# Mixer of a decoder trunk: the exponentials of the first query block turned by VectorE and sixteen DMAs

## The chip, the cores and the metric

One Trainium2 chip, one of its cores. The metric is the device time of one execution in microseconds; lower is better. The kernel before takes 979.72 us (median of 3 runs, 979.69 to 980.86).

## The reference, cut to what matters

The model is two layers of SwiGLU, mixer, SwiGLU over 256 positions of width 1024, all in float32. Only the mixer's dilated half is touched. For each of 8 heads of width 64 it is, as the kernel computes it in one piece:

```python
s = (q @ k.T) / sqrt(64) + log(multiplicity of the key in three dilated windows)   # -inf where none
p = exp(s - max(s))
o = (p @ v) / sum(p)
```

Queries come in two blocks of 128. Block 0 sees keys 0 to 127 (8 tiles of 128x128 exponentials, one per head), block 1 sees keys 0 to 255 (16 tiles). TensorE wants the exponentials with the keys on the partitions for the product with v, so each 128x128 tile has to be turned.

## The kernel before, in words

Weights come in loads of 1 MB (`load`, lines 240, 247, 233), all issued from SyncE's queue into three rotating buffers named raw. ScalarE casts each half of a load to a high part (`hi`, lines 272 and 276), VectorE subtracts to get a low part (`lo`, lines 272 and 277; at two places GpSimd does), and TensorE multiplies in three passes. One `tick` is one such split, of half a load.

The mixer first projects: 96 steps (`STEPS`) of TensorE matmuls (lines 700 to 702 and 305 to 307, output pj_m), six chunks of 16 steps, then the out-projection as steps 96 and up. All other work is hung behind these steps by hand in the table `PLAN`; the order on TensorE, VectorE and ScalarE is exactly the order of the program. The order on SyncE's queue is not written by hand: a scheduler sets it when the program is built, from priorities and from when it believes a transfer's buffer is free. A load is asked for by the first tick that needs it. In the mixer's second half these are the ticks of steps 50, 58, 65 and 73 for the last four loads of w_in (each serves two ticks: 50 and 53, 58 and 61, 65 and 68, 73 and 75), and steps 83, 92, 98 and 101 for w_out.

Around the change: `scores` (line 763) and `expos` (lines 779, VectorE, and 780, ScalarE) make exponentials of block 1 at step 36 and of block 0 at step 46. Block 1 is turned without TensorE: `flip` (line 817) transposes every 32x32 square in place on VectorE, at steps 44 and 47, and `carry` (line 827) moves the squares to their places by 16 DMAs between SBUF addresses, at steps 48 to 63. Block 0 is turned at step 53 by `turn_p`: eight TensorE transposes (line 810) into two PSUM tiles and two ScalarE copies (line 812). Both results are read by `attend_dil` (line 857), block 0 first at step 94. Between them lie `rope` at steps 56 and 64 (lines 728 to 730), the scores of the differential half at steps 68 and 75, their exponentials in `expos`, `differ` (lines 789 to 797) and `turn_p` of that half at steps 77 to 83.

SBUF is given out by hand in rooms: exponentials of the dilated half lie in E (block 0) and B (block 1), those of the differential half in E (block 0) and A (block 1), the turned tiles in F and C. Room D holds the rotated q and k of the differential half.

Of the kernel before, what the change touches and what calls it, by code (L numbers as in the profile page):

```python
# [11 lines left out]
F32 = mybir.dt.float32  # L12
# [8 lines left out]
P = 128  # L21
# [6 lines left out]
NH_DIL = 8  # L28
# [3 lines left out]
NT = S // P  # L32
# [13 lines left out]
def _two_pi_parts():  # L46
# [18 lines left out]
PLAN = {  # L65
    8: "tick",
    10: "norm",
    11: "tick tick",
    13: "tick",
    16: "table",  # L70
    17: "rope,0,0 rope,0,1",
    19: "tick",
    21: "tick",
# [5 lines left out]
    35: "tick",  # L79
    36: "score,dil,1 exp,dil,1,0 exp,dil,1,2 exp,dil,1,1 exp,dil,1,3",  # L80
    40: "rope,2,0",
    44: "flip,0 flip,2",
    43: "tick",
    45: "tick",
    46: "score,dil,0 exp,dil,0,0 exp,dil,0,2 exp,dil,0,1 exp,dil,0,3",
    47: "flip,1 flip,3",
    48: "rope,2,1",
    50: "tick",
    53: "turnp,dil,0,0 turnp,dil,0,1 tick",
    56: "rope,3,0",  # L90
    58: "tick",
    61: "tick",
# [32 lines left out]


for _n in range(16):
    PLAN[48 + _n] = f"{PLAN.get(48 + _n, '')} carry,{_n}"


@with_exitstack
def trunk_kernel(ctx: ExitStack, tc: tile.TileContext, a: dict, out: bass.AP):
    nc = tc.nc
# [11 lines left out]
    def trb(name):  # L145
        return pp.tile([P, 512], F32, tag="tr", name=name, bufs=2)
# [4 lines left out]
    def room(tag, shape, dt, name):  # L151

        return big.tile([P, *shape], dt, tag=f"room{tag}", name=name)
# [514 lines left out]
    def mixer(l, nx, cs, consts, nxt):  # L668
        nm = f"m{l}"
# [17 lines left out]
        vs, es, dens, PT, prs, mrg, pjs, outs, scs, qk = ({} for _ in range(10))  # L687
# [44 lines left out]
        def late(t):  # L732

            if "late" not in prs:
                prs["late"] = room("B", [4, 512], F32, f"late_{nm}")
            return prs["late"][:, t]
# [29 lines left out]
        def expos(fam, t, i):  # L766

            nk = (t + 1) * P
            mask = consts[f"mask_{fam}"]
            if (fam, t) not in es:  # L770
                es[fam, t] = room("EB"[t] if fam == "dil" else "EA"[t], [8, nk], F32, f"ex{fam}{t}_{nm}")
                if fam == "dif":
                    dens[t] = spool.tile([P, 8], F32, tag="den", name=f"den{t}_{nm}", bufs=2)
            s3, mk = scs.pop((fam, t, i)), mask[:, (2 - t - 1) * P:]
            mx = spool.tile([P, 2], F32, tag="mx", name=f"mx{fam}{t}{i}_{nm}", bufs=4)
            for g in range(2):
                h = 4 * g + i
                e = expo_of(fam, t, h)
                V.tensor_tensor_reduce(e, s3[:, g], mk, -(HD ** -0.5), 3e38, ALU.add, ALU.min, mx[:, g:g + 1])
                A.activation(e, e, AF.Exp, bias=mx[:, g:g + 1], scale=-1.0,  # L780
                             accum_out=dens[t][:, h:h + 1] if fam == "dif" else None)

        def expo_of(fam, t, h):
            return es[fam, t][:, h]
# [14 lines left out]

        def turn_p(fam, t, b, copies="a"):  # L800

            heads = range(NH_DIL) if fam == "dil" else range(0, 8, 2)
            if (fam, t) not in prs:
                prs[fam, t] = room("FC"[t], [2 * (t + 1), 512], F32, f"PTdil{t}_{nm}") if fam == "dil" else None
            o = prs[fam, t][:, b] if fam == "dil" else late(t + b)
            o = o.rearrange("p (k c) -> p k c", c=P)
            blocks = [(h, kt) for h in heads for kt in range(t + 1)][4 * b:4 * b + 4]
            tp = trb(f"trp{fam}{t}{b}_{nm}")
            for i, (h, kt) in enumerate(blocks):
                T.transpose(tp[:, i * P:(i + 1) * P], expo_of(fam, t, h)[:, kt * P:(kt + 1) * P], ident)  # L810
                PT[fam, t, h, kt] = o[:, i]
            COPY[copies](o, tp.rearrange("p (k c) -> p k c", c=P))

        def flip(i):

            e = es["dil", 1][:, i::4]
            V.transpose(e, e)

        def carry(n):

            if not n:
                prs["dil", 1] = room("C", [2 * NH_DIL, P], F32, f"PTdil1_{nm}")
                for b in range(2 * NH_DIL):
                    PT["dil", 1, b // 2, b % 2] = prs["dil", 1][:, b]
            f, t = n // 4, n % 4
            e = es["dil", 1].rearrange("p h (k c) -> p (h k) c", c=P)
            nc.sync.dma_start(prs["dil", 1][t * 32:(t + 1) * 32, :, f * 32:(f + 1) * 32],
                              e[f * 32:(f + 1) * 32, :, t * 32:(t + 1) * 32])

        def attend_dif(t):  # L830
            p3 = outs["ps", t] = scb(f"avf{t}_{nm}").rearrange("p (h e) -> p h e", e=2 * HD)
# [36 lines left out]
        def merge(fam, t):  # L868
# [12 lines left out]
            else:  # L881
                A.activation(mh, t3, AF.Copy, scale=gain[:, 0:1])
                V.scalar_tensor_tensor(ml, t3, gain[:, 0:1], mh.bitcast(F32), op0=ALU.mult, op1=ALU.subtract)

        JOBS = {"norm": nx.scale, "table": tables, "rope": rope, "score": scores, "exp": expos, "differ": differ,
                "turnp": turn_p, "value": value, "avdif": attend_dif, "avdil": attend_dil, "ndif": norm_dif,
                "ndil": norm_dil, "flip": flip, "carry": carry,
                "merge": merge, "tick": lambda low="v": ticks(1, low)}

# [172 lines left out]
```

## Time and profile before

| | us |
|---|---|
| median of 3 runs | 979.72 |
| the profiled execution | 979.83 |
| its span, first to last instruction | 978.0 |
| TensorE busy | 967.5 (99%) |
| VectorE busy | 713.4 (73%) |
| ScalarE busy | 550.8 (56%) |
| DMA queue of the loads and carries, share of 16 engines | 57.9% |

All rows come from the one profiled execution. Each row gives the start in us from the span's start, then the duration, the engine, the line and what the instruction writes and reads. Matmuls are pipelined, so a matmul's cost in a stream is the distance of its start from the next one's, not its duration. The first layer's mixer runs its second half from about 236 to 290 us, the second layer's from about 716 to 770 us.

### The profile page before, as it was taken

To read this page: it belongs to the slowest core of one execution; us is meant where nothing else is said; L and a number is where in the kernel's file an instruction comes from. 1 tells how busy PE (TensorE), PEld (TensorE's weight loads), DVE (VectorE), ACT (ScalarE), POOL (GpSimd) and SP (SyncE) were. 2 spreads that over 40 slices of the span, in tenths; PEclk is the share of its full clock that TensorE was granted. 3 is DMA by queue.
4 is the path that set the end of the run, shared out by engine and by line. 5 is a ranking of instruction groups with operands and counts; after the bars stand their busy time and mean duration, and the time that the engine had idled before them with its cause. 6 is when DMAs were issued, how large, how long until landed. Compare 5 with 4: busy or idle time off the path is not lost.

```text
span 978.0 us, 15500 instructions
## 1 busy us (share of the span) xinstructions
PE 967.5 (99%) x5947; PEld 854.2 (87%) x5947; DVE 713.4 (73%) x1290; ACT 550.8 (56%) x982; POOL 57.1 (6%) x63
## 2 busy tenths in 40 slices
PE   8999999999999999999999999999999999999997
PEld 7888888899888888888888888889998988888886
DVE  6887788689668877775478777665986789777542
ACT  7765655355656665564357656554447566665532
POOL 0000000010212000000010000001002120000000
PEclk9999999999999999999999999999999999999999
DMA  9965566635635666466646566653654656855531
GB/s 291 274 213 187 158 197 205 215 127 160 189 112 179 205 207 202 163 209 199 215 151 193 174 194 204 206 192 110 215 143 135 197 173 190 240 174 199 188 130 44
DMA packets 159691, 179.96 MB, mean 184 GB/s; under 512 B 30288, under 2 KB 122624, under 8 KB 159616
## 3 DMA queue, kind: packets, MB, share of 16 engines
q1 hardware_dynamic: 159440, 178.69, 57.9%
q8 instruction: 47, 0.77, 0.3%
q10 hardware_dynamic: 176, 0.27, 0.1%
q14 instruction: 28, 0.23, 0.1%
HBM read 174.75 MB, written 1.05 MB: 180 GB/s over the span
## 4 chain that ended last, share of the span: by engine, by line
PE 92%; DVE 4%; ACT 2%; issue 1%; DMA 0%; SPq 0%; POOLq 0%; POOL 0%; ACTq 0%
PE u_f L373 8%; PE g_f L373 8%; PE dnf L373 8%; PE u_s L373 8%; PE g_s L373 7%; PE g_f L370 4%; PE u_f L370 4%; PE dnf L370 4%; PE dns L373 4%; PE u_s L370 4%; PE g_s L370 4%; PE pj_m L700 3%; PE pj_m L701 3%; PE pj_m L702 3%; PE dns L370 2%; DVE lo L277 2%
## 5 line engine op out<-in xcount | busy, mean ns | idle before, releaser
L277 DVE TENSOR_TENSOR lo<-raw,hi 128x1024 fp32r<-128x1024 f32 (+1 forms) x293 | 353.5, 1225 | 134.7 <-ACT hi L276 133.8
L276 ACT CAST hi<-raw 128x1024 fp32r<-128x1024 f32 (+1 forms) x297 | 303.4, 1046 | 124.3 <-PE u_f L373 26.8
L373 PE MATMUL u_s<-xs_s,hi 128*128 128x512 f32 x352 | 127.3, 395 | 0.0
L373 PE MATMUL g_s<-xs_s,hi 128*128 128x512 f32 x352 | 127.0, 394 | 0.0
L370 PE MATMUL g_s<-xs_s,lo 128*128 128x256 f32 x352 | 91.7, 281 | 0.0
L370 PE MATMUL u_s<-xs_s,lo 128*128 128x256 f32 x352 | 91.5, 280 | 0.0
L373 PEld LDWEIGHTS u_s<-xs_s,hi 128*128 128x128 f32 x352 | 66.0, 187 | 11.2
L373 PEld LDWEIGHTS g_s<-xs_s,hi 128*128 128x128 f32 x352 | 66.0, 188 | 11.0
L700 PE MATMUL pj_m<-xs_m,hi 128*128 128x256 f32 x256 | 72.8, 284 | 0.0
L702 PE MATMUL pj_m<-xs_m,lo 128*128 128x256 f32 x256 | 71.6, 280 | 0.0
L701 PE MATMUL pj_m<-xs_m,hi 128*128 128x256 f32 x256 | 71.6, 280 | 0.0
L370 PEld LDWEIGHTS g_s<-xs_s,lo 128*128 128x128 f32 x352 | 66.5, 189 | 3.9
L370 PEld LDWEIGHTS u_s<-xs_s,lo 128*128 128x128 f32 x352 | 66.5, 189 | 3.9
L373 PE MATMUL g_f<-xs_in,hi 128*128 128x512 f32 x176 | 65.1, 401 | 0.0
L373 PE MATMUL u_f<-xs_in,hi 128*128 128x512 f32 x176 | 64.8, 400 | 0.0
L373 PE MATMUL u_f<-xs_f,hi 128*128 128x512 f32 x176 | 63.7, 395 | 0.0
L373 PE MATMUL g_f<-xs_f,hi 128*128 128x512 f32 x176 | 63.5, 394 | 0.0
L700 PEld LDWEIGHTS pj_m<-xs_m,hi 128*128 128x128 f32 x256 | 48.1, 188 | 1.0 <-issue 0.7
L701 PEld LDWEIGHTS pj_m<-xs_m,hi 128*128 128x128 f32 x256 | 48.2, 188 | 0.1
L702 PEld LDWEIGHTS pj_m<-xs_m,lo 128*128 128x128 f32 x256 | 48.1, 188 | 0.0
L272 ACT CAST hi<-raw 128x1024 fp32r<-128x1024 f32 x32 | 31.5, 1046 | 25.5 <-PE pj_m L701 9.3
L272 DVE TENSOR_TENSOR lo<-raw,hi 128x1024 fp32r<-128x1024 f32 x32 | 38.4, 1235 | 10.3 <-ACT hi L272 10.3
(361 smaller groups left out, 2203.6 us busy)
## 6 DMA issues: line engine op xcount, KB each, us to landing
raw<-in_ffn_gate_dram SPq DMA_DIRECT2D x86, 512.0 KB, 4.1
raw<-in_ffn_up_dram SPq DMA_DIRECT2D x86, 512.0 KB, 5.2
raw<-in_ffn_down_dram SPq DMA_DIRECT2D x41, 1024.0 KB, 5.1
raw<-in_w_in_dram SPq DMA_DIRECT2D x24, 1024.0 KB, 5.2
raw<-in_w_out_dram SPq DMA_DIRECT2D x8, 1024.0 KB, 6.3
raw<-in_ffn_down_dram SPq DMA_DIRECT2D x6, 512.0 KB, 3.6
PTdil_m<-exdil_m SPq DMA_DIRECT2D x32, 64.0 KB, 2.3
xt<-turned SPq DMA_DIRECT2D x16, 64.0 KB, 5.2
```

The costliest lines, as they stand in the source:

```text
L272: out = [lambda: A.copy(hi, raw), lambda: ENGINE[low].tensor_sub(lo, raw, hi.bitcast(F32))]
L276: out.append(lambda sl=sl: A.copy(hi[:, sl], raw[:, sl]))
L277: out.append(lambda sl=sl: ENGINE[low].tensor_sub(lo[:, sl], raw[:, sl], hi[:, sl].bitcast(F32)))
L370: T.matmul(ps[:, :S], wl, xs[:, 0], start=False, stop=False)
L373: T.matmul(ps, wh, xs.rearrange("p j s -> p (j s)"), start=start, stop=stop)
L700: T.matmul(ps, hi, nx.xs[k][:, 0], start=k == 0, stop=False)
L701: T.matmul(ps, hi, nx.xs[k][:, 1], start=False, stop=False)
L702: T.matmul(ps, lo, nx.xs[k][:, 0], start=False, stop=k == KD - 1)
```

## The change

Block 0 of the dilated exponentials is turned as block 1 is. `turnp,dil,0,0` and `turnp,dil,0,1` leave step 53; two flips of four heads each come in at step 54; sixteen carries of block 0 come in at steps 64 to 79 (those of block 1 stay at 48 to 63). The exponentials of the differential block 0 move from room E to room D, since room E is now read by the carries until they are done. `flip` and `carry` take the block as an argument, and `turn_p` keeps only the differential half.

```diff
-    53: "turnp,dil,0,0 turnp,dil,0,1 tick",
+    53: "tick",
+    54: "flip,0,0 flip,0,1",
...
 for _n in range(16):
-    PLAN[48 + _n] = f"{PLAN.get(48 + _n, '')} carry,{_n}"
+    for _t in range(NT):
+        PLAN[64 - 16 * _t + _n] = f"{PLAN.get(64 - 16 * _t + _n, '')} carry,{_t},{_n}"
...
-                es[fam, t] = room("EB"[t] if fam == "dil" else "EA"[t], [8, nk], F32, f"ex{fam}{t}_{nm}")
+                es[fam, t] = room("EB"[t] if fam == "dil" else "DA"[t], [8, nk], F32, f"ex{fam}{t}_{nm}")
...
+        def flip(t, i):
+
+            e = es["dil", t][:, i::4] if t else es["dil", t][:, 4 * i:4 * i + 4]
             V.transpose(e, e)
...
+        def carry(t, n):
 
             if not n:
+                prs["dil", t] = room("FC"[t], [NH_DIL * (t + 1), P], F32, f"PTdil{t}_{nm}")
+                for b in range(NH_DIL * (t + 1)):
+                    PT["dil", t, b // (t + 1), b % (t + 1)] = prs["dil", t][:, b]
+            f, to = n // 4, n % 4
+            e = es["dil", t].rearrange("p h (k c) -> p (h k) c", c=P)
+            nc.sync.dma_start(prs["dil", t][to * 32:(to + 1) * 32, :, f * 32:(f + 1) * 32],
+                              e[f * 32:(f + 1) * 32, :, to * 32:(to + 1) * 32])
```

A carry of block 0 moves 32 partitions x 8 heads x 32 elements, 32 KB in runs of 128 bytes; one of block 1 moves twice as much.

## Rows read from the trace of the kernel before

**Rows 1.** The page: busy time by engine, and the chain that ended last.

```profile
PE 967.5 (99%) x5947; PEld 854.2 (87%) x5947; DVE 713.4 (73%) x1290; ACT 550.8 (56%) x982; POOL 57.1 (6%) x63
...
PE 92%; DVE 4%; ACT 2%; issue 1%; DMA 0%; SPq 0%; POOLq 0%; POOL 0%; ACTq 0%
```

**Rows 2.** Busy time in one stretch: PE, PEld, DVE, ACT, POOL, clock, DMA, GB/s.

```profile
236.00:290.00 54.00, 54.00 (x387) 47.28 (x386) 36.51 (x88) 29.91 (x65) 8.65 (x6) 1.00 0.51 149
```

**Rows 3.** TensorE in order of time at step 53; then all transposes of line 810.

```profile
237.37 0.28 PE L701 MATMUL pj_m<-xs_m,hi 128*128 128x256 f32 x1
237.49 0.28 PE L702 MATMUL pj_m<-xs_m,lo 128*128 128x256 f32 x1
...
238.60 0.28 PE L701 MATMUL pj_m<-xs_m,hi 128*128 128x256 f32 x1
...
L810 PE MATMUL trpdil_m<-ident,exdil_m x16: 271/272/273, 237.6 to 718.7; 128*128 128x128 f32 x16
```

**Rows 4.** By tile: flips, with ns min/median/max, first and last start.

```profile
L817 DVE STREAM_TRANSPOSE exdil_m<-exdil_m x8: 669/688/709, 230.2 to 715.3; 128x512 f32<-128x512 f32 x8
```

**Rows 5.** ScalarE in order of time, with the idle before and its releaser.

```profile
238.24 1.07 ACT L812 COPY PTdil_m<-trpdil_m 128x512 f32<-128x512 f32 x2 [1.85 <-PE trpdil_m L810]
239.20 2.96 ACT L276 CAST hi<-raw 128x1024 fp32r<-128x1024 f32 x3
```

**Rows 6.** VectorE in order of time, steps 50 to 64.

```profile
237.47 1.22 DVE L277 TENSOR_TENSOR lo<-raw,hi 128x1024 fp32r<-128x1024 f32 x1
240.29 1.23 DVE L277 TENSOR_TENSOR lo<-raw,hi 128x1024 fp32r<-128x1024 f32 x1 [1.61 <-ACT hi L276]
241.44 0.68 DVE L728 TENSOR_TENSOR qkdif_m<-pj_m,csr_m 128x512 f32<-128x512 f32 x1
...
247.04 1.53 DVE L730 TENSOR_TENSOR qkdif_m<-qkdif_m,turn_m 128x512 f32<-128x512 f32 x1
```

**Rows 7.** TensorE in order of time: the scores of step 68.

```profile
249.11 2.01 PE L763 MATMUL scdif_m<-qkdif_m 32*128 32x256 f32 x32
```

**Rows 8.** SyncE's queue in order of time: carries, the next load, both layers.

```profile
235.72 11.88 SPq L827 DMA_DIRECT2D PTdil_m<-exdil_m  x16
247.70 0.57 SPq L240 DMA_DIRECT2D raw<-in_w_in_dram  x1
...
716.01 10.71 SPq L827 DMA_DIRECT2D PTdil_m<-exdil_m  x16
```

**Rows 9.** SyncE's queue at the start of the span: small transfers back to back.

```profile
1.73 0.43 SPq L233 DMA_DIRECT2D raw<-in_ffn_up_dram  x1
2.21 0.43 SPq L916 DMA_DIRECT2D xt<-in_x_dram  x1
```

**Rows 10.** By line: loads of w_in, all 24, from issue to landing.

```profile
DMA to landing us min/median/max: 5.0/5.2/7.0
```

**Rows 11.** SyncE's queue in the last up-projection: groups of four like carries, and loads.

```profile
822.27 2.69 SPq L558 DMA_DIRECT2D xt<-turned  x4
825.85 0.37 SPq L233 DMA_DIRECT2D raw<-in_ffn_gate_dram  x1
...
826.81 3.58 SPq L558 DMA_DIRECT2D xt<-turned  x4
...
834.32 0.37 SPq L233 DMA_DIRECT2D raw<-in_ffn_gate_dram  x1
...
835.29 6.11 SPq L558 DMA_DIRECT2D xt<-turned  x4
```

**Rows 12.** The chain from step 73's cast: ScalarE, VectorE, TensorE.

```profile
256.13 1.03 ACT L276 CAST hi<-raw 128x1024 fp32r<-128x1024 f32 x1
...
257.82 1.22 DVE L277 TENSOR_TENSOR lo<-raw,hi 128x1024 fp32r<-128x1024 f32 x1
...
263.83 0.73 PE L810 MATMUL trpdif_m<-ident,exdif_m 128*128 128x128 f32 x4
```

**Rows 13.** TensorE in order of time: the first reader of block 0's turned tiles.

```profile
275.68 0.78 PE L857 MATMUL avl_m<-vdil_m,PTdil_m 128*128 128x65 f32 x6
```

## What I predicted before seeing the change

> **What bounds the kernel now.** I read the page first: TensorE is busy for 967.5 us of a span of 978.0, and 92% of the chain that ended last is TensorE's [rows 1]. [...] So a microsecond taken from TensorE's stream is a microsecond of the kernel, if nothing that TensorE reads comes later than it does now. The other rows are for that "if": who hands TensorE its operands, and how much time each has to spare.
>
> **What goes.** The eight transposes of step 53. One ordinary matmul starts 0.12 us after the other (237.37, 237.49); across the transposes the second matmul behind starts at 238.60 [rows 3]. That is 1.11 us where two ordinary distances would be 0.24, so the transposes cost 0.87 us. Sixteen transposes in all [rows 3], eight in each layer: 1.74 us of TensorE. The matmul behind them waits for nothing else there, so I count all of it. With them go two ScalarE copies, 1.07 us, and the 1.85 us that ScalarE stood still ahead of them for TensorE [rows 5].
>
> **What VectorE gets.** Two flips per layer of 128x512, as wide as those of block 1, at 0.69 us [rows 4]: 1.38 us, at step 54. VectorE is in order, and behind the flips stand the rope of step 56, two splits, the rope of step 64 and, at TensorE, the scores of step 68, which read both ropes. The flips are covered by VectorE's idle 1.61 us ahead of the split at 240.29 [rows 6]. That idle comes from ScalarE's cast, which started only at 239.20, behind the copies [rows 5]. Without copies the cast can follow the one of step 50 at once, so that the split runs from 238.7 to 239.9, the flips to 241.2, and the rope starts at 241.2 instead of 241.44. From there to the end of the last rope's add at 248.57 (247.04 + 1.53) is 7.13 us, so it ends by 248.33. TensorE wants its scores at 249.11 [rows 7] less 0.87, at 248.24. This fits to 0.1 us per layer, an upper end, since a part of those 7.13 us was waiting for TensorE, which is now earlier; I take nothing. If the cover were gone, the add would end 1.38 us later than before, at 249.95, and TensorE would wait 1.7 us per layer.
>
> Room D for the exponentials of the differential block 0 adds a wait for the scores of step 75, their last reader; those exponentials are made from these very scores, so it costs nothing.
>
> **What the DMA queue gets.** Sixteen carries per layer on SyncE's queue, each with an issue time, and behind them whatever the queue holds. Their own result has time: TensorE reads it at 275.68 [rows 13]. What hasn't is the last load of w_in, which the splits of steps 73 and 75 need. In before it leaves at 247.70, right behind the sixteen carries of block 1 [rows 8]. Its buffer is freed by the split of step 53, that ends at 241.5 [rows 6], so it is the carries that hold it, and it shows that a ready load does not overtake carries that stand earlier in the program. The up-projection shows the same: the four groups of four transfers of line 558 are ready together, once VectorE's transposes are done, yet loads that stand between them in the program leave between them, at 825.85 and up to 834.32, and the third group only after those, at 835.29 [rows 11]. The queue follows the program's order among what it believes ready. For the change this means: nine of the new carries (those of steps 64 to 72) ahead of the load of step 73, seven behind it. The loads of steps 50 to 65 leave before the carries of block 1 and are not touched.
>
> The issue of a carry of block 0 is not in the trace. Carries of block 1 with twice the runs take 11.88/16 = 0.74 us each in one layer and 10.71/16 = 0.67 in the other [rows 8]; small transfers back to back at the start go out every 0.48 us, with 0.43 us each in the issue alone [rows 9]. The issue may be a fixed price or grow with the runs; I take 0.48, half the runs being nearest to those small transfers, and keep 0.43 and 0.74 for the range. A gain is excluded, since the queue only gets longer.
>
> So in the first layer the load leaves at 247.70 + 9 x 0.48 = 252.0 and lands, at the median of 5.2 us (5.0 to 7.0, [rows 10]), at 257.2. When is it needed? The cast of step 73 started at 256.13, but VectorE took it up only at 257.82 [rows 12], behind its own work. With TensorE 0.87 us earlier that is 256.95, less the cast's 1.03 us: it may land at 255.9 for nothing. It is 1.3 us late. In the second layer the carries of block 1 end at 726.72, 246.43 on the first layer's scale, so the load leaves at 250.85, lands at 256.05 and is 0.15 us late.
>
> **Who waits for that.** ScalarE and VectorE are in order: behind the cast and the split of step 73 stand the exponentials of the differential block 0, then `differ`, then TensorE's transposes of step 83 at 263.83, which took 0.73 us instead of running straight through [rows 12]; they already wait for `differ` by a little. There is no slack in this chain, so each microsecond of lateness is one of TensorE. 1.3 + 0.15 = 1.45 us come back.
>
> **The sum**: -1.74 + 1.45 = -0.3 us on the profiled execution's 979.83, its span of 978.0 and 1.83 around it. That execution lies 0.11 us above the median of the runs, so 979.4 us. With 0.43 and 5.0 us the two layers are 0.7 and 0 late: net -1.0, 978.7. With 0.74 and 0.67 they are 3.7 and 1.9 late: net +3.8, 983.5. What else moves: the loads of w_out leave some 7 us later than before, but the first is cast only for step 83 and has that much to spare.
>
> **The rivals.**
>
> *The load leaves first.* The split of step 53, which frees its buffer, stands ahead of the flips in VectorE's order, so the scheduler may believe the load ready before the carries. For it: that order. Against: it then has to believe the queue free too, and [rows 11] say that it reckons such carries as long. Nothing comes back: 979.72 - 1.74 = 978.0 us.
>
> *All sixteen carries go ahead of the load* (slower). One mechanism, one place: the load of step 73 lands after 255.9. 247.70 + 16 x 0.48 + 5.2 = 260.6 is 4.7 us late, in the second layer 3.5. Net +6.5, 986.2 us. It decides from the point where both layers together are 1.74 us late. For it: in before all sixteen of block 1 go ahead. Against: seven of the new ones stand behind that tick in the program.
>
> *The flips lie on the path*: ScalarE's cast doesn't move forward because something else holds it. 2 x 1.7 - 1.74 = +1.7, 981.4 us. Against: the cast follows its neighbour without a gap in [rows 5], once the copies are done.
>
> *The long way is too long.* In before the turned tiles are ready at 239.3 [rows 5]; now flips, queue and landings bring them to about 258, and TensorE reads them at 275.68 [rows 13]. Only if they came 17 us later still would this make it slower, to 981 and up. [...]
>
> **How the numbers follow.** About 0.2% (2.0 us) is what a measurement of this kernel can tell from no change. Nine carries ahead: 0.56, of which 0.14 with the upper half of its bounds, slower by over 2 us; the rest within. Load first: 0.22, just inside 0.2%, and with any small wait that goes as well outside, so half and half. Sixteen ahead: 0.10. Flips: 0.05, the long way: 0.02, both about at the limit. The 0.05 left is a gain that I don't see. Faster 0.16, same 0.55, slower 0.29. The range goes from the load-first case, 977.8, to just above the upper bound, 984.0.
>
> **What would show it.** In the changed trace: no line 810 into trpdil, matmuls 0.12 us apart through step 53; the flips ahead of a rope at 241.2; nine carries, then the load of w_in, then seven. The queue's rows give the carry's true issue time; the idle ahead of step 73's cast, released by a DMA, and TensorE's pause at step 83 must be the same length. I am wrong if the load stands elsewhere in the queue, or if TensorE pauses at the scores of step 68.

## The result: 0.8% slower, and the profile after

| | before | after |
|---|---|---|
| median, us | 979.71 (979.33 to 980.86, 6 runs) | 987.76 (987.11 to 989.23, 6 runs) |
| profiled execution, us | 979.83 | 987.57 |
| its span, us | 978.0 | 985.8 |

The ratio is 1.0082, with an interval of 1.0071 to 1.0094. I had forecast 979.4 us, between 977.8 and 984.0: the sign is wrong and the time lies above the range. In the changed kernel all lines behind `PLAN` stand two further down or up: the casts are L278, the splits L279, the transposes L808, their copies L810, the flips L815, the carries L825, the last loads L242 and L249. In e3 and e5 further down two more lines stand ahead, so that the transposes are L810 there and their copies L812.

**The page after**: busy time by engine, then the chain that ended last.

```profile
PE 970.7 (98%) x5931; PEld 856.1 (87%) x5931; DVE 715.8 (73%) x1294; ACT 549.1 (56%) x978; POOL 56.5 (6%) x63
...
PE 89%; DVE 4%; ACT 4%; DMA 2%; issue 1%; SPq 0%; POOLq 0%; POOL 0%; ACTq 0%
```

Sixteen matmul instructions are gone, as they should be (5947 in [rows 1], 5931 here), and yet TensorE is busy for longer: 970.7 instead of 967.5 us. Its share of the chain fell by 3 points, ScalarE's rose by 2, and DMA came in with 2% where it had 0%. So there are two things to find: a transfer that something waits for, and matmuls that take longer.

**SyncE's queue after**, in order of time, both layers (start, duration, engine, line, what, count).

```profile
235.53 17.41 SPq L825 DMA_DIRECT2D PTdil_m<-exdil_m  x25
253.04 0.55 SPq L242 DMA_DIRECT2D raw<-in_w_in_dram  x1
253.63 4.98 SPq L825 DMA_DIRECT2D PTdil_m<-exdil_m  x7
...
719.90 17.76 SPq L825 DMA_DIRECT2D PTdil_m<-exdil_m  x25
737.76 0.55 SPq L242 DMA_DIRECT2D raw<-in_w_in_dram  x1
```

Twenty-five carries, the load, seven carries: sixteen of block 1 and exactly nine of block 0 ahead of the load of step 73, in both layers. That is the order that I had worked out. But the load leaves at 253.04, where [rows 8] had it at 247.70 and I had put it at 252.0. In the second layer it is worse: the queue's first carry there starts 484.37 us after the first layer's, so on the first layer's scale the load leaves at 253.39, where I had 250.85.

**The chain that ended last, after**, from that load to TensorE (start, duration, what).

```profile
253.04 6.02 DMA raw<-in_w_in_dram
...
259.14 1.05 ACT hi L278
...
260.22 1.23 DVE lo L279
...
261.69 3.19 ACT exdif_m L782 x16
264.88 0.96 ACT late_m L810 x2
...
265.88 1.02 PE trpdif_m L808 x4
```

This is the road that I had named: the load, the cast and the split of step 73, the exponentials of the differential block 0, the transposes of step 83. One link is another than I had: where I put `differ`, the trace puts the last wait down to two ScalarE copies of tiles turned earlier (264.88 to 265.84), which stand behind the exponentials in ScalarE's order. They come late for the same reason. The cast of [rows 12] stood at 256.13, now it stands at 259.14.

**TensorE after, in order of time**, at step 83 and behind it (in brackets the idle time ahead, and who ended it).

```profile
262.55 0.40 PE L309 MATMUL pj_m<-hi,xs_m 128*128 128x512 f32 x1
265.88 1.02 PE L808 MATMUL trpdif_m<-ident,exdif_m 128*128 128x128 f32 x4 [2.93 <-ACT late_m L810]
266.66 0.48 PE L307 MATMUL pj_m<-hi,xs_m 128*128 128x512 f32 x1
...
267.52 0.63 PE L307 MATMUL pj_m<-hi,xs_m 128*128 128x512 f32 x1
267.95 0.63 PE L308 MATMUL pj_m<-lo,xs_m 128*128 128x512 f32 x1
```

TensorE stands still for 2.93 us. Then comes what I had not thought of: from 267.52 on, 1.6 us behind the pause, the matmuls start 0.43 us apart, where ordinary ones start 0.23 to 0.24 apart.

**Busy time in two stretches after**: us, PE, PEld, DVE, ACT, POOL, clock, DMA share, GB/s.

```profile
262.90:265.90 3.00, 0.07 (x2) 0.05 (x1) 1.15 (x8) 3.00 (x14) 0.79 (x1) 1.00 1.04 397
...
267.50:270.08 2.58, 2.58 (x8) 1.98 (x6) 1.23 (x1) 0.97 (x2) 0.00 (x0) 0.50 0.60 223
```

In the pause the clock is still granted in full (1.00). In the second stretch it is granted at 0.50. Finer windows of the same view put the edges at 267.3 and 270.75, so the half clock lasts 3.4 us, and 3.4 us again in the second layer (0.50 from 752.0 to 755.4). TensorE works all that time, with matmuls 0.43 us apart instead of 0.23 to 0.24: this is where its busy time grows.

**Who TensorE waited for, after**, by tile and releaser: us in all, times, longest.

```profile
PE trpdif_m L808 <- ACT late_m L810: 5.8, 2, 2.9
```

Once per layer, 5.8 us together.

**The balance.** It goes by starts on TensorE. First two rows of before: the first matmul behind step 83's transposes and the first behind the first group of `attend_dif`, step 86. Then the changed kernel: the scores of step 68, and again the first matmul behind that group.

```profile
264.32 0.47 PE L305 MATMUL pj_m<-hi,xs_m 128*128 128x512 f32 x1
...
267.31 0.48 PE L305 MATMUL pj_m<-hi,xs_m 128*128 128x512 f32 x1
...
248.05 2.01 PE L765 MATMUL scdif_m<-qkdif_m 32*128 32x256 f32 x32
...
271.21 0.48 PE L307 MATMUL pj_m<-hi,xs_m 128*128 128x512 f32 x1
```

The scores of step 68 start at 248.05, those of [rows 7] at 249.11: 1.06 us earlier, of which 0.19 because everything starts earlier (235.53 against 235.72). So the transposes gave back 0.87 us. The first matmul behind step 83's transposes starts at 266.66, in before at 264.32: 2.34 later, so that the pause took 2.34 + 1.06 = 3.40 us. The first matmul behind that group of `attend_dif` starts at 271.21, in before at 267.31: 3.90 later, so that the slow clock took 3.90 - 2.34 = 1.56 us. The first layer then loses -0.87 + 3.40 + 1.56 = 4.09 us, and indeed the second layer's carries start 484.37 us after the first layer's instead of 480.29 (716.01 - 235.72, [rows 8]), 4.08 later. The second layer, read by the same three starts (732.43, 750.96 and 755.53, in before 729.49, 744.70 and 747.71), begins 3.90 behind and loses -0.96 + 3.32 + 1.56 = 3.92. Together that is 8.0 us: the 7.8 between the spans and the 0.19 of the earlier start.

The idle of 2.93 us is thus 0.47 less than what the pause took: the transposes behind it spread over 1.02 us instead of the 0.73 of [rows 12], and the ends of the matmuls ahead are modelled. For pauses read from idle time I therefore add 0.47 each; the second layer's 2.86 becomes 3.3, as its starts say too.

### The profile page after: what moved, and what is told of

Its sections match the earlier page's. It is cut to its first block, busy times and chain, and to the rows that moved or that the text cites. A ratio compares the mean times of both kernels' runs of the same rounds, so it can differ in the third digit from the quotient of the medians.

```text
span 985.8 us, 15506 instructions
## 1 busy us (share of the span) xinstructions
PE 970.7 (98%) x5931; PEld 856.1 (87%) x5931; DVE 715.8 (73%) x1294; ACT 549.1 (56%) x978; POOL 56.5 (6%) x63
## 4 chain that ended last, share of the span: by engine, by line
PE 89%; DVE 4%; ACT 4%; DMA 2%; issue 1%; SPq 0%; POOLq 0%; POOL 0%; ACTq 0%
PE g_f L375 8%; PE u_f L375 8%; PE dnf L375 8%; PE u_s L375 7%; PE g_s L375 7%; PE g_f L372 4%; PE u_f L372 4%; PE dnf L372 4%; PE dns L375 4%; PE u_s L372 4%; PE g_s L372 4%; PE pj_m L702 3%; PE pj_m L703 3%; PE pj_m L704 3%; DVE lo L279 2%; PE dns L372 2%
## 5 line engine op out<-in xcount | busy, mean ns | idle before, releaser
L279 DVE TENSOR_TENSOR lo<-raw,hi 128x1024 fp32r<-128x1024 f32 (+1 forms) x293 | 353.4, 1226 | 138.2 <-ACT hi L278 136.7
L278 ACT CAST hi<-raw 128x1024 fp32r<-128x1024 f32 (+1 forms) x297 | 303.1, 1046 | 136.1 <-PE u_f L375 27.1
L375 PEld LDWEIGHTS u_s<-xs_s,hi 128*128 128x128 f32 x352 | 66.1, 188 | 11.1
L372 PE MATMUL g_f<-xs_in,lo 128*128 128x256 f32 x176 | 46.2, 283 | 0.0
L372 PE MATMUL u_f<-xs_in,lo 128*128 128x256 f32 x176 | 45.9, 281 | 0.0
```

Of the source, the lines that this page charges most:

```text
L278: out.append(lambda sl=sl: A.copy(hi[:, sl], raw[:, sl]))
L279: out.append(lambda sl=sl: ENGINE[low].tensor_sub(lo[:, sl], raw[:, sl], hi[:, sl].bitcast(F32)))
L372: T.matmul(ps[:, :S], wl, xs[:, 0], start=False, stop=False)
L375: T.matmul(ps, wh, xs.rearrange("p j s -> p (j s)"), start=start, stop=stop)
```

## The experiments

The theory after the result: SyncE's queue makes the load late, TensorE pauses at step 83 for as long as the load is late, and the pause brings a stretch of half clock with it. A first rival: flips, rooms or the longer way of the tiles cost the time, and the queue only looks guilty. A second: the half clock comes from something else that the change brings, such as the denser DMA traffic, and not from the pause.

| run | place of block 0's carries | its time, us | before on the same chip, us | ratio, interval |
|---|---|---|---|---|
| e1_behind | steps 74 to 89, all behind the load | 978.29 (11 runs) | 980.39 (21 runs) | 0.998, 0.9971 to 0.9989 |
| e2_five | steps 68 to 83, five ahead | 980.70 (10 runs) | 980.39 | 1.0006, 0.9997 to 1.0015 |
| the change | steps 64 to 79, nine ahead | 987.76 (6 runs) | 979.71 (6 runs) | 1.0082, 1.0071 to 1.0094 |
| e4_sixteen | steps 57 to 72, all ahead | 996.06 (one run) | 980.39 | none |
| e3_fill | as the change, 7 matmuls in the pause | 990.25 (4 runs) | 980.39 | 1.0099, 1.0086 to 1.0113 |
| e5_fill3 | as the change, 3 matmuls in the pause | 985.50 (4 runs) | 980.26 (7 runs) | 1.0053, 1.0036 to 1.007 |
| e7_pool | as the change, issued by GpSimd | 978.91 (one run) | 980.26 | none |
| e6_probe | as e1, and 24 unread transfers | 977.59 (one run) | 980.26 | none |

### All carries of block 0 behind the load

```diff
-        PLAN[64 - 16 * _t + _n] = f"{PLAN.get(64 - 16 * _t + _n, '')} carry,{_t},{_n}"
+        PLAN[(48 if _t else 74) + _n] = f"{PLAN.get((48 if _t else 74) + _n, '')} carry,{_t},{_n}"
```

> The changed kernel with one edit: the carries of block 0 stand at steps 74 to 89 instead of 64 to 79, so that all sixteen come behind the load of step 73 in SyncE's queue. Theory of the queue: the load leaves at about 247.5 again, TensorE has no pause at step 83 and the clock stays at 1.00; what is left of the change is the 0.87 us per layer taken from TensorE: 979.7 - 1.7 = 978.0 us. Rival, that the carries and flips cost what they cost wherever they stand: 985 us or more, with the lost time somewhere else than at step 83.

978.29 us. Flips, rooms, carries and the long way are all there, and the loss is not only gone: the kernel is 2.1 us faster than before. SyncE's queue in this kernel, in order of time, first layer; then step 73's cast and the transposes of step 83; then busy time in the stretch of [rows 2], with its columns:

```profile
236.50 11.71 SPq L825 DMA_DIRECT2D PTdil_m<-exdil_m  x16
248.31 0.57 SPq L242 DMA_DIRECT2D raw<-in_w_in_dram  x1
248.99 7.49 SPq L825 DMA_DIRECT2D PTdil_m<-exdil_m  x9
...
256.04 1.99 ACT L278 CAST hi<-raw 128x1024 fp32r<-128x1024 f32 x2
...
263.75 0.68 PE L808 MATMUL trpdif_m<-ident,exdif_m 128*128 128x128 f32 x4
...
236.00:290.00 54.00, 54.00 (x386) 47.28 (x385) 38.51 (x91) 29.77 (x64) 8.98 (x6) 1.00 0.63 165
```

The load leaves 11.81 us behind the first carry, in before 11.98 [rows 8]. No idle stands ahead of the cast or the transposes, TensorE is busy for the whole stretch and the clock is 1.00. The first rival falls: only the place in the queue is different. The kernel moves as many bytes as the changed one, and from 267.50 to 270.08 its DMA share is 1.02 with the clock at 1.00, where the changed kernel has 0.60 and 0.50. So traffic as dense as that did not bring the clock down here. The gain, 1.1 to 2.8 us by the interval, fits what I had priced the sixteen transposes at, 1.74.

The way by VectorE and the DMA queue is the longer one (the last carry of block 0 goes out by 261.69 us, where the copies of before were done at 239.31, [rows 5]), and yet the run speaks for it: in this stretch TensorE has no idle time (busy for 54.00 of 54.00 us) and VectorE has (38.51 of 54.00), and the time is 978.29 us against 980.39.

### Five or sixteen ahead of the load

The same line with 68, and with 57, in the place of 74.

> The changed kernel with the carries of block 0 at steps 68 to 83: five of them ahead of the load of step 73 instead of nine. Theory of the queue: four issues of 0.69 us less, so the load is 2.8 us earlier, and of the pause of about 3.4 us per layer some 0.6 us stay; if the clock falls only behind a long pause, 979.7 - 1.7 + 1.2 = 979.2 us; if any pause costs its 1.6 us of clock, 982.4 us. Rival, that the carries cost the same wherever they stand: 987 us.

> The changed kernel with the carries of block 0 at steps 57 to 72: all sixteen ahead of the load of step 73. Theory of the queue: seven issues of 0.69 us more, 4.8 us per layer on top: 987.8 + 9.7 = 997 us, a pause of about 8 us at step 83. Rival, that the carries cost the same wherever they stand: 987 us.

With five ahead 980.70 us, not to be told from before. SyncE's queue; step 73's cast; who TensorE waited for at step 83; and busy time behind it:

```profile
235.81 14.99 SPq L825 DMA_DIRECT2D PTdil_m<-exdil_m  x21
250.90 0.55 SPq L242 DMA_DIRECT2D raw<-in_w_in_dram  x1
...
256.97 1.99 ACT L278 CAST hi<-raw 128x1024 fp32r<-128x1024 f32 x2 [1.52 <-DMA raw<-in_w_in_dram]
...
PE trpdif_m L808 <- ACT late_m L810: 1.3, 2, 0.8
...
266.00:272.00 6.00, 6.00 (x40) 5.35 (x39) 3.52 (x6) 3.14 (x5) 1.04 (x2) 1.00 0.57 209
```

Twenty-one carries in 14.99 us: the load is late by a little, TensorE pauses 0.8 and 0.5 us, and behind the first layer's pause, the one of 0.5 us, the clock stays at 1.00; its mean over the whole execution is 0.999, in before 0.998 and in the changed kernel 0.996. I had expected 979.2, with less of a pause. With 0.47 added to each, the sum is -1.8 + 1.3 + 0.9 = +0.4 us, and the span is 978.4, 0.4 above before's.

With sixteen ahead 996.06 us in one run. SyncE's queue; the transposes of step 83; the waits; busy time inside the pause and behind it:

```profile
236.31 22.77 SPq L825 DMA_DIRECT2D PTdil_m<-exdil_m  x32
259.18 0.55 SPq L242 DMA_DIRECT2D raw<-in_w_in_dram  x1
...
271.40 1.17 PE L808 MATMUL trpdif_m<-ident,exdif_m 128*128 128x128 f32 x4 [7.68 <-ACT late_m L810]
...
PE trpdif_m L808 <- ACT late_m L810: 14.3, 2, 7.7
...
267.00:271.30 4.30, 0.00 (x0) 0.00 (x0) 2.45 (x20) 4.08 (x19) 2.18 (x1) 0.56 0.68 227
...
271.00:274.00 3.00, 2.60 (x8) 2.14 (x9) 1.12 (x5) 2.32 (x4) 0.00 (x0) 0.50 0.88 341
```

Thirty-two carries in 22.77 us, 0.71 each; pauses of 14.3 us in all, and behind the first layer's the half clock again (0.50 from 271.0 to 274.0). Time and pause are about what I had expected (997 us, 8 us). Between 267.0 and 271.3, inside the pause, the granted clock is 0.56 on the mean: it falls while TensorE does nothing (0.00 us busy in that window). Over the four kernels the order is one of dose: 0, 5, 9 and 16 carries ahead of the load give pauses of 0, 1.3, 5.8 and 14.3 us. Take the spans' differences to before's 978.0 (-1.2, 0.4, 7.8 and 16.2 us), take off what the first carry starts later than in before (0.8, 0.1, -0.2 and 0.6), add the 1.8 of the transposes and take off the pauses with 0.47 each: what stays is -0.2, -0.1, 3.1 and 2.2 us. The two kernels whose clock stays up have next to nothing left over, the two with the half clock 2 to 3. With sixteen ahead it is less, since a part of the half clock falls into the pause, where TensorE has no work to lose.

### Matmuls in the pause

```diff
-    83: "turnp,dif,0,0 tick",
+    83: "fill turnp,dif,0,0 tick",
...
+        def fill():
+            for _ in range(7):
+                T.matmul(pjs[5, 0], zeros, dg, start=False, stop=False)
```

They add products with zeros to an open sum, so nothing else changes; the carries stay where the change puts them. If TensorE's standing still is what brings the clock down, it should stay up with the pause filled, though the load is as late as ever.

> The changed kernel, carries where they are, with seven matmuls added on TensorE just ahead of the transposes of step 83, where it pauses: zeros as weights, 512 columns, added onto an accumulation that is running, so that the sums stay the same. They are to take about 0.44 us each, 3.1 us in all, as long as the pause. Theory that the loss has two parts, the pause and the lower clock behind it: the pause stays (TensorE waits for the same copies) but the clock stays at 1.00 through step 86, which gives back about 1.6 us per layer: 987.8 - 3.1 = 984.6 us. Rival, that the slow matmuls behind the pause have another cause than the pause (the loads and carries that land then): the matmuls stay 0.43 us apart there, 987.8 us.

990.25 us: my fill was too long. TensorE in order of time:

```profile
263.45 6.17 PE L887 MATMUL pj_m<-dilg,zeros 128*128 128x512 f32 x14
269.46 0.60 PE L810 MATMUL trpdif_m<-ident,exdif_m 128*128 128x128 f32 x4
```

Each of the seven ran as two passes of 0.43 us, fourteen in all, and the transposes waited for them instead of for ScalarE: what the clock gave back went into the fill, and the time says nothing on it. The trace does: from 269.5 to 275.0, behind the fill, the clock is 1.00. So once more with three:

> The same fill with three added matmuls instead of seven. Each ran as two passes of 0.43 us, so seven took 6.0 us and outlasted the pause; three take 2.6 us, less than the pause of 3.4 us, so they add nothing of their own. If the clock's fall behind the pause is a cost of its own, it stays at 1.00 and the run is 1.6 us per layer faster than the changed kernel, 987.8 - 3.1 = 984.6 us; if what is lost is the pause alone, 987.8 us.

985.50 us, 5.24 above before instead of the change's 8.05. TensorE in order of time, and busy time behind step 83:

```profile
263.21 2.74 PE L887 MATMUL pj_m<-dilg,zeros 128*128 128x512 f32 x6
266.94 1.02 PE L810 MATMUL trpdif_m<-ident,exdif_m 128*128 128x128 f32 x4 [1.00 <-ACT late_m L812]
...
267.72 0.48 PE L309 MATMUL pj_m<-hi,xs_m 128*128 128x512 f32 x1
...
270.71 0.48 PE L309 MATMUL pj_m<-hi,xs_m 128*128 128x512 f32 x1
...
266.90:272.00 5.10, 5.06 (x29) 4.24 (x30) 2.36 (x6) 3.00 (x5) 0.00 (x0) 1.00 0.63 230
```

The transposes come no earlier than in the changed kernel (266.94 against 265.88), and TensorE waits out the load's lateness as it does there, 2.74 us on zeros and 1.00 idle. But behind it the clock is 1.00. From the first matmul behind these transposes to the first behind that group of `attend_dif` it takes 2.99 us (267.72 to 270.71), as in before (264.32 to 267.31), where the changed kernel took 4.55 (and 4.57 in its second layer). The carries and their place ahead of the load are those of the change; only TensorE's standing still is shorter. So here it was the standing still that brought the half clock: with 2.93 us of it the clock fell to 0.50, with 1.00 us it stayed at 1.00. The clock cost the changed kernel 1.56 us in each layer, 3.1 in both. The medians say 8.05 - 5.24 = 2.8 us, with a wide margin: e5's interval alone is 3.5 to 6.9 us above before. What stays in e5 is the lateness. In the first layer the transposes start 3.73 us behind the zeros' first start (263.21 to 266.94) and spread over 1.02 us instead of 0.73, so zeros and idle together took 4.0 us. In the second layer the idle is 0.4 us instead of 1.0 (1.4 in both), so I estimate 3.4 there. -1.8 + 4.0 + 3.4 = 5.6, and its span is 5.8 above before's.

### The same carries from another queue

```diff
-            nc.sync.dma_start(prs["dil", t][to * 32:(to + 1) * 32, :, f * 32:(f + 1) * 32],
+            (nc.sync if t else nc.gpsimd).dma_start(prs["dil", t][to * 32:(to + 1) * 32, :, f * 32:(f + 1) * 32],
```

> The changed kernel with the carries of block 0 at the same steps, issued from GpSimd's queue instead of SyncE's. Theory of the queue: the load of step 73 leaves at 247.5 as before, no pause at step 83, 978 us; GpSimd's two splits of a low part stand in the same queue behind eight carries each and may come late, which would show as a wait for them at steps 82 and 86. Rival, that the transfers themselves slow the load: it leaves at 247.5 but lands at 257 or later, 982 us and up.

One run, 978.91 us. All carries of block 0, both layers, on GpSimd (ns min/median/max, first and last start); then the load in SyncE's queue, and GpSimd's split of that load's second half:

```profile
L825 POOL DMA_DIRECT2D PTdil_m<-exdil_m x32: 582/582/775, 242.0 to 732.8; - x32
...
248.17 0.57 SPq L242 DMA_DIRECT2D raw<-in_w_in_dram  x1
...
258.08 3.12 POOL L279 TENSOR_TENSOR lo<-raw,hi 128x1024 fp32r<-128x1024 f32 x1 [4.30 <-ACT hi L278]
```

With the steps of `PLAN` as the change has them, but no carry of block 0 in SyncE's queue, the load leaves 12.18 us behind the first carry and no pause is left at step 83 (0.2 us at one layer's scores of step 68 is the only new wait of TensorE there; it waits for none of GpSimd's splits). The same transfers are issued beside the same load, and what the load feeds comes no later: GpSimd's split of its second half starts at 258.08, in before at 258.19, in the changed kernel at 261.21. So here it is not their traffic but their place ahead of the load that cost the time. What the other queue saves is the time of the issues ahead of the load, and that is no small time here: in the changed kernel nine of them take 6.1 us, and the load lands 6.0 us after its own start.

### What a carry's issue costs

This kernel is e1 with 24 more transfers between two halves of an input tile that is no longer read, four alike of each of six kinds (four of the kinds here). They stand in the first layer's second up-projection; the queue started them earlier, from 112 to 200 us.

```diff
+                nc.sync.dma_start(pdst[to, 0:256], psrc[of, 0:256])                  # L1007
...
+                nc.sync.dma_start(dst[to, 0:4, 0:32], src[of, 0:4, 0:32])            # L1009
...
+                nc.sync.dma_start(dst[to, 0:8, 0:32], src[of, 0:8, 0:32])            # L1011
...
+                nc.sync.dma_start(dst[to, 0:16, 0:32], src[of, 0:16, 0:32])          # L1013
```

> The kernel with the carries at steps 74 to 89, and 24 transfers added that nobody reads, from one part of xt to another, in groups of four alike: 32 partitions with 1 run of 1 KB, with 4, 8 and 16 runs of 128 bytes; 128 partitions with 2 runs of 128 bytes (256 runs, as in a carry of block 0); 128 partitions with 1 run of 256 bytes. Only the issue times on SyncE's queue are looked at, not the run's time. If the price is fixed for a transfer between SBUF addresses: 0.6 to 0.7 us for all. If it goes by runs: 0.37 for one run, 0.4 for 4, about 0.65 for 8 and 1.2 for 16 (but carries of block 1, with 16 runs, took 0.63 here). If it goes by the number of dimensions of the pattern: the two with one run per partition near 0.37, the others near 0.63.

SyncE's queue by line: count, ns min/median/max of one issue, first and last start.

```profile
L1007 SPq DMA_DIRECT2D xt<-xt x4: 582/590/612, 112.4 to 114.3; - x4
L1009 SPq DMA_DIRECT2D xt<-xt x4: 585/592/672, 115.0 to 117.7; - x4
L1011 SPq DMA_DIRECT2D xt<-xt x4: 592/597/604, 176.8 to 187.2; - x4
L1013 SPq DMA_DIRECT2D xt<-xt x4: 586/606/642, 187.9 to 192.7; - x4
...
L242 SPq DMA_DIRECT2D raw<-in_w_in_dram x24: 367/368/567, 171.3 to 725.7; - x24
```

One run of 1 KB on each of 32 partitions, or 4, 8 or 16 runs of 128 bytes: 0.59 to 0.61 us each at the median. The two kinds on 128 partitions took 0.60 (one run of 256 bytes) and 0.66 (two runs of 128 bytes; the longest of these four 1.37). So in this run the issue of a transfer from SBUF to SBUF is close to a fixed price, 0.59 to 0.66 us, as the first of the three expectations had it; half the runs do not make it cheaper (0.60 for 8, 0.61 for 16). A load of 1 MB from memory takes 0.37, and 0.55 right behind carries (the rows above).

## Why the prediction was wrong, step by step

**Right: what goes.** 0.87 us of TensorE in the first layer and 0.96 in the second, seen at the scores of step 68, and in e1's time.

**Right: the flips are covered.** They ran from 239.54 for 1.30 us, where I had 239.9 to 241.2, and TensorE does not wait at the scores of step 68. Room D and the longer way cost nothing: in e1 both are there, and TensorE has no idle time.

**Right: the queue's order and the chain.** Nine carries, the load, seven carries; cast, split, exponentials, transposes, with ScalarE's two copies for `differ` as the last link; and no slack in that chain. It fits to a tenth: by my working the load might land at 255.9 for nothing, at 255.7 with the earlier start. It landed at 259.06, 3.36 late, and the pause took 3.40. Of my signs, one failed: the idle time ahead of step 73's cast is 3.96 us, longer than the pause, because ScalarE stood still from 255.18 on. Neither sign of being wrong came, the load elsewhere in the queue or a pause at step 68: both were signs of the path, and neither could have shown a wrong price.

**Wrong, the issue of a carry (0.48 us).** This is the step that failed first. I let the price fall with the runs and took it from loads at the start of the span [rows 9], which come from memory; I called them small, but they move 128 KB each, four times a carry of block 0. It was 0.68 in the first layer: the first sixteen carries take 11.33 us of the 17.41 (the first row below), so nine take 6.1. In the second layer seventeen take 11.46 of the 17.76 (the second row), so the last eight take 6.3, 0.79 each. The nearest row was at hand: a carry of block 1, 0.67 to 0.74 in [rows 8], the same instruction from SBUF to SBUF. By that row alone I would have had my upper bound, 983.5, and the other sign. The queue of the changed kernel, cut at its sixteenth carry and at the second layer's seventeenth:

```profile
235.53 11.33 SPq L825 DMA_DIRECT2D PTdil_m<-exdil_m  x16
...
719.90 11.46 SPq L825 DMA_DIRECT2D PTdil_m<-exdil_m  x17
```

**Wrong, the landing (5.2 us).** I took the median of 24 loads [rows 10], but it was 6.0 and 5.6 us, with the DMA share at 0.88 and 0.90 from its start to its landing. Here too the nearest row was at hand: in the trace of before this very load takes 6.1 us in the first layer (the row below) and 6.6 in the second. So the change did not stretch it, and my median was too short for it. What makes it longer than the median was not tried by itself.

```profile
raw<-in_w_in_dram SPq DMA_DIRECT2D x1, 1024.0 KB, 6.1
```

The two layers were 6.7 us late together, where I had 1.45. Of the difference the queue has some 3.9 us and the landing 1.2.

**Wrong, the second layer (0.15 us late).** I let it start with the lead of [rows 8], where its block 1 took 10.71 instead of 11.88. The dearer carries took that lead back, and it was 3.3 us late: on the first layer's scale its load landed at 743.36 - 484.37 = 258.99.

**Missing, the clock.** I counted each microsecond of lateness as one of TensorE and gave no reason why the clock, 1.00 in [rows 2], should stay there behind a pause: no term of the sum, and no rival, had TensorE run slower there. It is worth 1.56 us in each layer, 3.1 in both. Without it the result would have been some 985 us, still above the range by a little.

**The sum again** with what was measured: -0.87 - 0.96 + 3.40 + 3.32 + 1.56 + 1.56 = +8.0, against 7.8 between the spans, 8.0 with the earlier start, and 8.05 between the medians.

**The rivals.** All sixteen ahead I had put at 986.2; the run gave 996.06. It has the same two errors in it, the price of the issue (with e1's 11.71 us for block 1, sixteen of block 0 take 22.77 - 11.71 = 11.1 us, not 7.7) and the clock. The load first I had put at 978.0; e1 has that order, by another place in `PLAN`, and gave 978.29. In my spread of chances the mistake was to hold the upper half of the bounds of one term for a quarter of a case, 0.14 of 0.56, although it rested on the row most like the new instruction.

## What to carry to other kernels

SyncE's queue kept the order of the program here for loads and small transfers alike: each carry put ahead of the load of step 73 made that load later by an issue, 0.68 to 0.79 us. Read that price from the transfer most like it (same kind, same two memories), and the time to landing from the very load that will wait, not from a median. When a load feeds a chain without slack, put the small transfers behind it in the program: the same change then wins 0.2% instead of losing 0.8%. Another queue did as well, in one run (978.91 against 980.26 us). And a pause of TensorE was not priced by its length alone: behind 2.9 us of idle the half clock cost 1.56 us more, behind 1.0 us (e5) nothing. Look at the granted clock behind it.

## What I had not expected of the hardware

- Behind a pause of 2.9 us that TensorE entered at full clock, it kept full clock for 1.5 us from its first transpose on, then ran 3.4 us at the granted clock of 0.50, and lost 1.56 us more in the first layer; in the second layer 1.8 and 3.4 us, and 1.56 lost again. In the pause of 7.7 us (e4) the clock fell while TensorE stood still: 1.00 from 263.7 to 267.0, 0.56 on the mean from 267.0 to 271.3. Behind the pause of 0.5 us in the first layer of e2 and behind 1.0 us of idle after the three zero matmuls in that of e5 the clock stayed at 1.00.
- An issue of a transfer between SBUF addresses takes 0.59 to 0.61 us at the median on SyncE's queue for 1 to 16 runs on each of 32 partitions (e6), and 0.58 on GpSimd for a carry of block 0 (e7); a load of 1 MB takes 0.37 (e6). In the changed kernel half of the 64 carries take 0.63 us or less and the longest takes 1.68; with gaps of 0.04 us or so between them that makes the 0.68 to 0.79 apiece. Why single ones take so long stays open.
